# Gated heads' values of all tokens: from eight jobs inside the halves to seven half-size products in a first stage

## The chip, the cores and the metric

The kernel runs on one core of a Trainium2 chip. The metric is the time of one execution on the device in microseconds, the median of several runs. Beside the runs there is one profiled execution, from which the page and all rows below come. TensorE multiplies, ScalarE and VectorE move, split and scale data, GpSimd adds operands that lie in SBUF, and the queue of SyncE (SP) issues nearly all DMA transfers.

## The reference, cut to what matters

A decoder layer on x of 1024 tokens by 2048 (float32). One input projection feeds two head groups; their gated outputs go through one output projection, a residual and a layer norm:

```python
h = jnp.einsum('bsd,de->bse', x, w_in[l])
q_a, k_a, v_a, z_a, q_g, k_g, v_g, z_g, gk_lr = jnp.split(h, pts, axis=-1)
y_a = _swa_sink_attention(qa, ka, va, attn_sinks[l]) * jax.nn.silu(z_a)   # 16 heads of 64, window 128
gk = log_sigmoid(gk_lr @ w_gk_up[l] + b_gk[l]) / 16
o_g = _gla_chunked(q_g, k_g, v_g, gk)                    # 4 gated heads, keys of 128, values of 256
y_g = rms_norm(o_g) * gla_norm_w[l] * jax.nn.silu(z_g)
x = _layer_norm(DN_ALPHA * x + concat([y_a, y_g]) @ w_out[l], ln_g[l], ln_b[l])
```

The change touches `v_g`: columns 3328 to 4352 of the projection, 1024 tokens x 2048 inputs x 1024 outputs.

## The kernel before, in words

**Precision.** Every large product is made of three matmuls: each operand is split into a high part (`A.copy` to float32r, L112) and a low remainder (`V.tensor_tensor` subtract, L113), and high x high, high x low and low x high are summed in PSUM. A split covers 128x512 and costs one ScalarE and one VectorE instruction. Loads land in tiles `raw` (4 buffers of 512 KB); split weights live in `w_p` (8 high, 8 low), split x in `x_p` (16 high, 16 low).

**Stages.** Two halves of 512 tokens, one after the other (`half_jobs`, L491), then an output stage. In a half, x is loaded and split once and stays; `begin` (L588) does that, with the first pair of jobs and the low-rank products of the decay (`low_rank`, L307). Then 38 jobs follow in the order of `ORDER` (L42). A job of kind f (`main_f`, L165) computes one block of 128 output columns for the half's 512 tokens: 16 k steps x 3 matmuls with weights held and x moving, 128x512 each. A job of kind v (`main_v`, L177) computes the 256 value columns of one gated head: 16 k steps x 4 token blocks x 3 matmuls with x held and weights moving, 128x256 each. There are 34 jobs of kind f and 4 of kind v in a half.

**What runs beside the jobs.** A job has an evacuation and a list `later`, whose entry n is run n jobs on (`run_later`, L648). For a gated head: after its key job (`k_job`, L511) come the decays and the operands of four near levels, a chain over ScalarE, VectorE and GpSimd; after its v job the values are split out of PSUM (L523, L524) and `near`, the products of these levels (`level_products`, L346), is due at once, then `far` one job on and two `pair` steps after that. For an attention job a (`qa`): the rotary step and the scores one job on. All of it is side work in the gaps of other engines; the scheduler puts its matmuls between those of the jobs. Every second job four loads, four GpSimd operations and a store prepare sums of output weights (`weight_sums`, L627).

**The output stage** (L818 on) is itself seven half-size products over 8 k steps, with y held and 512 weight columns moving, two column halves each. Sums of y are made by GpSimd from blocks loaded again (`y_part`, L708), one product ahead.

**Order.** A scheduler orders each engine's instructions by priority (program order, moved ahead inside `high_priority`) and by its own timing model; each engine and each queue then works strictly in that order. Before, the first loads of half 0 are pinned (`load_first`, L581), use a pool of their own (`x0`), and the low-rank products of half 0 come after the first pair.

Of the kernel before, what the change touches and what calls it, by code (L numbers as in the profile page):

```python
# [41 lines left out]
ORDER = [  # L42
    "K V q0 k0 v0 a0 z0 a1 z1 g0 h0 a2 z2 q1 k1 v1 a3 z3 g1 h1 a4 z4 q2 k2 v2 a5 z5 g2 h2 a6 z6 q3 k3 v3 a7 z7 g3 h3",
    "K V q0 k0 v0 a0 z0 a1 z1 g0 h0 a2 z2 q1 k1 v1 a3 z3 g1 h1 a4 z4 q2 k2 v2 a5 z5 g2 h2 a6 z6 q3 k3 v3 a7 z7 g3 h3",
]
# [30 lines left out]
def build(ctx: ExitStack, tc, xT, xr, w_e, w_v, w_gk, w_up, b_gk, cos_d, sin_d, cst_d, sinks, wn_d, w_out, g_d, b_d, out):  # L76
# [11 lines left out]
    ap = side.enter_context(tc.tile_pool(name="ap", bufs=1))  # L88
    so = side.enter_context(tc.tile_pool(name="so", bufs=1, space=PSUM))
    sd = side.enter_context(tc.tile_pool(name="sd", bufs=3, space=PSUM))  # L90

    x0 = ExitStack()
    x0_p = x0.enter_context(tc.tile_pool(name="x0", bufs=8))


    def load(src, pool=None, pieces=1, ahead=2000):

        r = (pool or raw_p).tile([P, 2, 512], F32, name="raw", tag="raw")
        v = src.rearrange("p (u c) -> p u c", u=2)
        with tc.high_priority(ahead):  # L100
            for i in range(pieces):
                u = slice(2 * i // pieces, 2 * (i + 1) // pieces)
                ins = SP.dma_start(r[:, u], v[:, u])
                if ahead == 0:
                    tc.keep_in_program_order(ins)
        return [r[:, 0], r[:, 1]]
# [9 lines left out]
    def load_split(src, pool, tag, ahead=2000):  # L116
        out = []
        for i in range(src.shape[-1] // 1024):
            out += [split(u, pool, tag) for u in load(src[:, 1024 * i:1024 * i + 1024], ahead=ahead)]
        return out  # L120
# [40 lines left out]
    ys_d = dr_p.tile([P, 8 * T], F32, name="ysum")  # L161
    yd = [[dr_p.tile([P, 4 * T], F32, name=f"yd{H}_{q}") for q in range(4)] for H in range(2)]
# [13 lines left out]

    def main_v(w, xs):  # L177
        acc = [mm.tile([P, 2, 256], F32, name="accv", tag="mm") for _ in range(2)]
        for k in range(KT):
            wh, wl = w[k // 2]  # L180
            c = slice((k % 2) * 256, (k % 2) * 256 + 256)
            xh, xl = xs[k]
            for tb in range(NB):
                o = acc[tb // 2][:, tb % 2]
                t = slice(tb * P, tb * P + P)
                PE.matmul(o, xh[:, t], wh[:, c], start=(k == 0 and tb % 2 == 0), stop=False, skip_group_check=True)  # L186
                PE.matmul(o, xh[:, t], wl[:, c], start=False, stop=False, skip_group_check=True)  # L187
                PE.matmul(o, xl[:, t], wh[:, c], start=False, stop=(k == KT - 1), skip_group_check=True)  # L188
        return acc
# [301 lines left out]
    def half_jobs(H):  # L491
# [19 lines left out]
        def k_job(hd):  # L511
            def evac(acc):
                A.copy(c["kq", hd][:, 0], acc)
                c["dd", hd] = decays(hd, c["lr"])
                c["ws", hd] = {h: level_operand(c["kq", hd], c["dd", hd], h) for h in NEAR}
            e_job(H, E_KG + hd, evac)

        def v_job(hd):
            def evac(acc):
                v = c["v", hd] = [gp.tile([P, NB, 256], F32R, name=f"vg{i}", tag=f"vg{i}") for i in range(2)]  # L520
                for i in range(2):
                    o = slice(2 * i, 2 * i + 2)
                    A.copy(v[0][:, o], acc[i])  # L523
                    V.tensor_tensor(v[1][:, o], acc[i], v[0][:, o].bitcast(F32), ALU.subtract)  # L524
# [11 lines left out]
            jobs.append(Job([w_v[hd][:, :2048], w_v[hd][:, 2048:]], H, "v", evac, (near, far, pair, pair)))  # L536
# [15 lines left out]
        make = {"K": ka, "V": va, "q": q_job, "k": k_job, "v": v_job, "g": lambda hd: zg(hd, 0), "h": lambda hd: zg(hd, 1), "a": qa, "z": za}  # L552
        for j in ORDER[H].split():
# [27 lines left out]
    def load_first(srcs):  # L581
        rs = [(p or raw_p).tile([P, 2, 512], F32, name="raw", tag="raw") for p in (x0_p, None, None)]
        for u in range(2):
            for r, src in zip(rs, srcs):
                tc.keep_in_program_order(SP.dma_start(r[:, u], src[:, 512 * u:512 * u + 512]))
        return [[r[:, 0], r[:, 1]] for r in rs]

    def begin(H, i):  # L588
# [5 lines left out]
        if H:  # L594
            with tc.high_priority(2000):
                c["wgk"] = cp.tile([P, KT * 32], F32, name="wgk", tag="lr")
                SP.dma_start(c["wgk"], w_gk)
        for q in range(4):
            for j in range(2):
                src = xT[H, q][:, 1024 * j:1024 * j + 1024]  # L600
                if H:
                    xr += load(src)
                elif q or j:
                    xr += load(src, x0_p, 1, 0)
                if j == 0 and q % 2 == 0:
                    ws = [jobs[i + n].src[0][:, 512 * q:512 * q + 1024] for n in range(2)]
                    if H or q:
# [304 lines left out]
```

## Time and profile before

| | |
|---|---|
| median of 3 runs | 1436.53 us (1434.97 to 1437.89) |
| profiled execution, its own time | 1435.88 us |
| its span | 1433.7 us |
| TensorE busy | 1414.9 us, 99% |
| VectorE / ScalarE / GpSimd busy | 856.7 / 600.3 / 290.3 us |
| bytes moved | 222.36 MB, 155 GB/s over the span |

A row of a timeline or of the chain begins with start and length in us. A matmul's length contains its way through the array, so consecutive matmuls overlap; the distance between starts is what one costs.

### The profile page before, as it was taken

Reading aid. Unit: us, or ns where it says so; the run is one execution under the profiler, and the core shown is the slowest. Engines: PE = TensorE matmul, PEld = TensorE weight load, DVE = VectorE, ACT = ScalarE, POOL = GpSimd, SP = SyncE. Lnnn points to the kernel's source line nnn. Section 1 sums busy time; section 2 is a strip of 40 time slices with the busy share of each in tenths; the row PEclk is TensorE's granted clock in tenths of the full one; section 3 lists DMA queues with packets and bytes.
Section 4 is the critical chain, followed back from the end, with each engine's and each line's share of the span. In section 5 each row is a group of like instructions: output and inputs, shape, how many; then the busy total and the mean of one; then the engine's idle time right before and its main releaser. Section 6 shows DMA issues by size and latency. Waiting matters only on the chain.

```text
span 1433.7 us, 23435 instructions
## 1 busy us (share of the span) xinstructions
PE 1414.9 (99%) x8992; PEld 1181.0 (82%) x8992; DVE 856.7 (60%) x1481; ACT 600.3 (42%) x1279; POOL 290.3 (20%) x325
## 2 busy tenths in 40 slices
PE   8999999999999999999999999999999999999996
PEld 5888889888888976898888888988898888888885
DVE  5565556555655566565655555564566645466798
ACT  5544435435443445344435443443545324433320
POOL 0032212221311122213212221131101412122000
PEclk9999999999999999999999999999999999999998
DMA  8243344443434435543443334433325797665552
GB/s 318 86 148 128 111 147 131 135 133 107 144 131 134 133 127 175 168 157 113 159 133 123 115 131 136 138 112 118 104 95 163 239 362 230 216 218 189 172 208 117
DMA packets 99231, 222.36 MB, mean 155 GB/s; under 512 B 10800, under 2 KB 43568, under 8 KB 97968
## 3 DMA queue, kind: packets, MB, share of 16 engines
q1 hardware_dynamic: 97968, 218.78, 46.1%
q10 hardware_dynamic: 1152, 2.10, 0.4%
q8 instruction: 70, 1.15, 0.3%
q14 instruction: 41, 0.34, 0.1%
HBM read 180.47 MB, written 35.65 MB: 151 GB/s over the span
## 4 chain that ended last, share of the span: by engine, by line
PE 98%; DVE 1%; DMA 1%; ACT 0%; POOL 0%; SPq 0%; issue 0%; DVEq 0%; POOLq 0%
PE acc L172 18%; PE acc L174 18%; PE acc L173 17%; PE acco L742 7%; PE acco L743 7%; PE acco L744 7%; PE accv L186 4%; PE accv L188 4%; PE accv L187 4%; PE po L291 2%; PE pa L360 1%; PE ps L259 1%; PE ps L260 1%; PE pt L281 1%; PE lracc L310 1%; PE pg L405 1%
## 5 line engine op out<-in xcount | busy, mean ns | idle before, releaser
L113 DVE TENSOR_TENSOR wl<-raw,wh 128x512 fp32r<-128x512 f32 x440 | 331.6, 759 | 280.7 <-ACT wh L112 258.1
L112 ACT CAST wh<-raw 128x512 fp32r<-128x512 f32 x440 | 269.8, 620 | 416.9 <-PE acc L173 283.5
L172 PE MATMUL acc<-xh,wh 128*128 128x512 f32 x1088 | 429.4, 396 | 6.5 <-ACT wh L112 6.5
L174 PE MATMUL acc<-xh,wl 128*128 128x512 f32 x1088 | 427.1, 393 | 0.0
L173 PE MATMUL acc<-xl,wh 128*128 128x512 f32 x1088 | 426.9, 393 | 0.0
L172 PEld LDWEIGHTS acc<-xh,wh 128*128 128x128 f32 x1088 | 205.0, 188 | 53.8 <-ACT wh L112 8.4
L174 PEld LDWEIGHTS acc<-xh,wl 128*128 128x128 f32 x1088 | 204.8, 188 | 44.8 <-issue 1.4
L173 PEld LDWEIGHTS acc<-xl,wh 128*128 128x128 f32 x1088 | 205.0, 188 | 42.6 <-issue 2.2
L743 PE MATMUL acco<-wl,xh 128*128 128x512 f32 x416 | 161.9, 389 | 0.0
L742 PE MATMUL acco<-wh,xh 128*128 128x512 f32 x416 | 160.7, 390 | 0.2
L744 PE MATMUL acco<-wh,xl 128*128 128x512 f32 x416 | 160.8, 389 | 0.0
L186 PE MATMUL accv<-wh,xh 128*128 128x256 f32 x512 | 145.3, 284 | 0.0
L188 PE MATMUL accv<-wh,xl 128*128 128x256 f32 x512 | 145.0, 283 | 0.0
L187 PE MATMUL accv<-wl,xh 128*128 128x256 f32 x512 | 144.8, 283 | 0.0
L186 PEld LDWEIGHTS accv<-wh,xh 128*128 128x128 f32 x512 | 98.1, 192 | 1.2 <-issue 0.7
L188 PEld LDWEIGHTS accv<-wh,xl 128*128 128x128 f32 x512 | 98.1, 192 | 0.6 <-issue 0.3
L187 PEld LDWEIGHTS accv<-wl,xh 128*128 128x128 f32 x512 | 98.2, 192 | 0.5
L742 PEld LDWEIGHTS acco<-wh,xh 128*128 128x128 f32 x416 | 78.1, 188 | 17.3 <-ACT xh L112 1.3
L744 PEld LDWEIGHTS acco<-wh,xl 128*128 128x128 f32 x416 | 78.1, 188 | 16.7 <-DVE xl L113 0.4
L743 PEld LDWEIGHTS acco<-wl,xh 128*128 128x128 f32 x416 | 78.1, 188 | 15.8
L113 DVE TENSOR_TENSOR xl<-yr,xh 128x512 fp32r<-128x512 f32 x56 | 38.5, 687 | 77.4 <-ACT xh L112 76.9
L112 ACT CAST xh<-yr 128x512 fp32r<-128x512 f32 x56 | 34.6, 620 | 118.4 <-POOL yr L721 66.9
(169 smaller groups left out, 1686.7 us busy)
## 6 DMA issues: line engine op xcount, KB each, us to landing
raw<-in_w_e_dram SPq DMA_DIRECT2D x134, 512.0 KB, 3.9
yr<-yd SPq DMA_DIRECT2D x88, 256.0 KB, 4.8
raw<-in_w_v_dram SPq DMA_DIRECT2D x32, 512.0 KB, 4.2
raw<-in_w_out_dram SPq DMA_DIRECT2D x128, 128.0 KB, 2.7
td<-raw SPq DMA_DIRECT2D x32, 512.0 KB, 3.5
raw<-td SPq DMA_DIRECT2D x32, 512.0 KB, 4.6
raw<-in_w_out_dram SPq DMA_DIRECT2D x24, 512.0 KB, 4.0
raw<-in_xT_dram SPq DMA_DIRECT2D x15, 512.0 KB, 4.7
```

Of the source, the lines that this page charges most:

```text
L112: A.copy(hi, src)
L113: V.tensor_tensor(lo, src, hi.bitcast(F32), ALU.subtract)
L172: PE.matmul(acc, wh[:, c], xh, start=(k == 0), stop=False)
L173: PE.matmul(acc, wh[:, c], xl, start=False, stop=False)
L174: PE.matmul(acc, wl[:, c], xh, start=False, stop=(k == KT - 1))
L186: PE.matmul(o, xh[:, t], wh[:, c], start=(k == 0 and tb % 2 == 0), stop=False, skip_group_check=True)
L187: PE.matmul(o, xh[:, t], wl[:, c], start=False, stop=False, skip_group_check=True)
L188: PE.matmul(o, xl[:, t], wh[:, c], start=False, stop=(k == KT - 1), skip_group_check=True)
L291: x = PE.matmul(po[64 * u:64 * u + 64, a:b], vt[:, j + 1, 64 * g:64 * g + 64], pms[u][:, a2:b2], start=(len(heads) < 2), stop=(j == NB - 1 ...
L742: PE.matmul(acc, yh[:, c], wh, start=(first and k == 0), stop=False, skip_group_check=True)
L743: PE.matmul(acc, yh[:, c], wl, start=False, stop=False, skip_group_check=True)
L744: PE.matmul(acc, yl[:, c], wh, start=False, stop=(last and k == 7), skip_group_check=True)
```

## The change

The values of all four gated heads and all 1024 tokens become one matrix product ahead of the halves. It is cut in two along tokens (T0, T1), inputs (K0, K1) and columns (F0, F1), and the four blocks of the result are made from seven products of half size instead of eight, with sums of blocks as operands (Winograd's form of Strassen's scheme). In the order in which they run:

| product | x operand | weight operand | goes to |
|---|---|---|---|
| 1 | T0K0 | K0F0 | kept in u1, and stays in the banks |
| 2 | T0K1 | K1F0 | added to 1 in the same banks: values of T0, F0 |
| 7 | T0K0 - T1K0 | K0F1 + K1F1 | u7 |
| 5 | T1K0 - T1K1, kept in `xsum` | K0F0 + K0F1, kept in `wsum` | u5 |
| 6 | `xsum` - T0K0 | `wsum` + K1F1 | u1, u7, u5, and values of T1, F1 |
| 4 | T1K1 | `wsum` + K1F0 | values of T1, F0 |
| 3 | `xsum` + T0K1 | K1F1 | values of T0, F1 |

The table gives the operations of the code below. Each product is 8 k steps x 4 token blocks x 3 matmuls of 128x512. Sums are made by GpSimd, x sums one product ahead; results go to DRAM (`vd`) and come back per head and half in the key job's evacuation, where they are split from SBUF instead of PSUM. `near` moves from the v job to one job after the key job. Half 0 now begins like half 1.

```diff
-ORDER = [
-    "K V q0 k0 v0 a0 z0 a1 z1 g0 h0 a2 z2 q1 k1 v1 a3 z3 g1 h1 a4 z4 q2 k2 v2 a5 z5 g2 h2 a6 z6 q3 k3 v3 a7 z7 g3 h3",
...
+ORDER = "K V q0 k0 a0 z0 a1 z1 g0 h0 a2 z2 q1 k1 a3 z3 g1 h1 a4 z4 q2 k2 a5 z5 g2 h2 a6 z6 q3 k3 a7 z7 g3 h3"
+    vd = [[dr_p.tile([P, NB, 512], F32, name=f"vd{H}_{F}") for F in range(2)] for H in range(2)]
...
-    def main_v(w, xs):
...
@@ k_job, evac
-            e_job(H, E_KG + hd, evac)
-
-        def v_job(hd):
-            def evac(acc):
+                r = raw_p.tile([P, NB, 256], F32, name="raw", tag="raw")
+                SP.dma_start(r, vd[H][hd // 2][:, :, hd % 2 * 256:hd % 2 * 256 + 256])
                 v = c["v", hd] = [gp.tile([P, NB, 256], F32R, name=f"vg{i}", tag=f"vg{i}") for i in range(2)]
-                for i in range(2):
-                    o = slice(2 * i, 2 * i + 2)
-                    A.copy(v[0][:, o], acc[i])
-                    V.tensor_tensor(v[1][:, o], acc[i], v[0][:, o].bitcast(F32), ALU.subtract)
+                A.copy(v[0], r)
+                V.tensor_tensor(v[1], r, v[0].bitcast(F32), ALU.subtract)
...
-            jobs.append(Job([w_v[hd][:, :2048], w_v[hd][:, 2048:]], H, "v", evac, (near, far, pair, pair)))
+            e_job(H, E_KG + hd, evac, (None, near, far, pair, pair))
...
@@ begin: load_first, the pool x0 and the late low-rank products of half 0 go; both halves do
+                with tc.high_priority():
+                    low_rank(c["lracc"], c["wgk"], k, xr[k])
...
+    vo = v_st.enter_context(tc.tile_pool(name="vo", bufs=5, space=PSUM))
...
+    xsum = [vp.tile([P, T], F32, name=f"xsum{k}") for k in range(8)]
+    wsum = [vp.tile([P, 2, 512], F32, name=f"wsum{k}") for k in range(4)]
+    us = {(i, t): vp.tile([P, 512], F32, name=f"u{i}{t}") for i in (1, 5, 7) for t in range(NB)}
...
+    def v_x(i, k):
...
+        if i in (1, 2, 4):
+            a = raw(*{1: (0, 0), 2: (0, 1), 4: (1, 1)}[i], "xh")
+        elif i == 7:
+            a = raw(0, 0, "xh")
+            G.tensor_tensor(a, a, raw(1, 0, "xl"), ALU.subtract)
+        else:
+            a = xsum[k]
+            if i == 5:
+                fetch(a, block(1, 0))
+            b = raw(*{5: (1, 1), 6: (0, 0), 3: (0, 1)}[i], "xl")
+            G.tensor_tensor(a, a, b, ALU.add if i == 3 else ALU.subtract)
+        return split(a, x_p, "x")
...
+    def v_w(i, kp):
...
+        if i in (1, 2, 3):
+            r = raw(*{1: (0, 0), 2: (1, 0), 3: (1, 1)}[i])
+        elif i == 7:
+            r = raw(0, 1)
+            G.tensor_tensor(r, r, raw(1, 1), ALU.add)
+        else:
+            r = wsum[kp]
+            if i == 5:
+                fetch(r, block(0, 0).rearrange("p (u c) -> p u c", u=2))
+            G.tensor_tensor(r, r, raw(*{5: (0, 1), 6: (1, 1), 4: (1, 0)}[i]), ALU.add)
+        return [split(r[:, u], w_p, "w") for u in range(2)]
...
+    def v_collect(i, t, acc):
+        u1, u5, u7 = (us[j, t] for j in (1, 5, 7))
+        if i == 1:
+            A.copy(u1, acc)
...
+        elif i == 6:
+            V.tensor_tensor(u1, u1, acc, ALU.add)
+            V.tensor_tensor(u7, u7, u1, ALU.add)
+            o = raw_p.tile([P, 512], F32, name="raw", tag="raw")
+            V.tensor_tensor(o, u5, u7, ALU.subtract)
+            SP.dma_start(vd[1][1][:, t], o)
+            V.tensor_tensor(u5, u5, u1, ALU.subtract)
+        else:
+            o = u7 if i == 4 else u5
+            V.tensor_tensor(o, o, acc, ALU.add)
+            SP.dma_start(vd[1 if i == 4 else 0][0 if i == 4 else 1][:, t], o)
+
+    v_seq = (1, 2, 7, 5, 6, 4, 3)
...
+        for k in range(8):
+            if (i, k) not in v_xs:
+                v_xs[i, k] = v_x(i, k)
+            if k % 2 == 0:
+                wv = v_w(i, k // 2)
+            if vn + 1 < len(v_seq):
+                v_xs[v_seq[vn + 1], k] = v_x(v_seq[vn + 1], k)
+            (xh, xl), (wh, wl) = v_xs[i, k], wv[k % 2]
+            for t in range(NB):
+                c = slice(t * P, t * P + P)
+                PE.matmul(v_acc[t], xh[:, c], wh, start=(k == 0 and i != 2), stop=False, skip_group_check=True)
+                PE.matmul(v_acc[t], xh[:, c], wl, start=False, stop=False, skip_group_check=True)
+                PE.matmul(v_acc[t], xl[:, c], wh, start=False, stop=(k == 7 and i != 1), skip_group_check=True)
+        for t in range(NB):
+            v_collect(i, t, v_acc[t])
...
-        if i > 5 and i % 2 == 0 and i // 2 - 3 < 32:
-            weight_sums(i // 2 - 3)
+        if i > 3 and i % 2 == 0 and i // 2 - 2 < 32:
+            weight_sums(i // 2 - 2)
```

The pools of the side work (`ap`, `gp`, and `so`, `sd` in PSUM) open only after the first stage has closed its own, on the same memory.

## Rows read from the trace of the kernel before

**Rows 1.** busy time per engine, from the page: us (share of the span) xinstructions
```profile
PE 1414.9 (99%) x8992; PEld 1181.0 (82%) x8992; DVE 856.7 (60%) x1481; ACT 600.3 (42%) x1279; POOL 290.3 (20%) x325
```

**Rows 2.** the chain that ended last, from the page, by engine
```profile
PE 98%; DVE 1%; DMA 1%; ACT 0%; POOL 0%; SPq 0%; issue 0%; DVEq 0%; POOLq 0%
```

**Rows 3.** windows of all engines: busy us and instructions, clock, DMA share, GB/s
```profile
core 0: us, PE busy (x) PEld busy (x) DVE busy (x) ACT busy (x) POOL busy (x), PEclk, DMA share, GB/s
0.00:20.00 20.00, 13.51 (x49) 9.54 (x50) 11.93 (x19) 12.84 (x22) 1.72 (x10) 1.00 0.89 328
1140.00:1160.00 20.00, 20.00 (x90) 16.57 (x89) 10.41 (x18) 5.36 (x9) 3.11 (x2) 1.00 1.04 396
1160.00:1180.00 20.00, 20.00 (x90) 16.58 (x89) 6.35 (x10) 4.82 (x9) 4.70 (x4) 1.00 1.02 347
...
243.00:256.00 13.00, 13.00 (x146) 10.36 (x137) 9.52 (x18) 6.30 (x11) 1.48 (x2) 1.00 0.47 163
...
60.00:530.00 470.00, 470.00 (x3416) 400.22 (x3415) 277.42 (x500) 208.48 (x458) 107.56 (x131) 1.00 0.40 130
```

**Rows 4.** TensorE by line, v jobs: xcount | busy us, mean ns | idle
```profile
L186 PE MATMUL accv<-wh,xh 128*128 128x256 f32 x512 | 145.3, 284 | 0.0
```

**Rows 5.** timeline of the first v job on TensorE: start us, us
```profile
63.87 0.28 PE L186 MATMUL accv<-wh,xh 128*128 128x256 f32 x1
...
71.43 0.28 PE L186 MATMUL accv<-wh,xh 128*128 128x256 f32 x1
```

**Rows 6.** timeline of the output stage on TensorE
```profile
1140.18 0.39 PE L742 MATMUL acco<-wh,xh 128*128 128x512 f32 x1
...
1172.82 0.39 PE L742 MATMUL acco<-wh,xh 128*128 128x512 f32 x1
```

**Rows 7.** windows of the low-rank products alone: TensorE busy us (x), clock, DMA
```profile
0.00:45.00 45.00, 6.13 (x32) 1.00 0.75 271
530.00:575.00 45.00, 8.42 (x32) 1.00 0.50 166
```

**Rows 8.** timeline of the start: the first matmul
```profile
6.49 0.80 PE L172 MATMUL acc<-xh,wh 128*128 128x512 f32 x1 [6.49 <-ACT wh L112]
```

**Rows 9.** by line and shape, splits and GpSimd: busy us, mean ns | idle
```profile
L112 ACT CAST wh<-raw 128x512 fp32r<-128x512 f32 x440 | 269.8, 620 | 416.9 <-PE acc L173 283.5 <-PE accv L188 55.6 <-issue 25.1
...
L113 DVE TENSOR_TENSOR xl<-raw,xh 128x512 fp32r<-128x512 f32 x40 | 26.5, 690 | 14.1 <-ACT xh L112 14.0
...
L208 POOL TENSOR_TENSOR rs<-rs,sin 128x512 f32<-128x512 f32 x18 | 31.8, 1769 | 97.3 <-DMA rs<-rq 97.2
...
L635 POOL TENSOR_TENSOR raw<-raw 128x256 f32<-128x256 f32 x32 | 24.5, 765 | 241.6 <-DMA raw<-in_w_out_dram 227.9 <-DVE wl L113 4.6 <-DVE sza L303 4.6
...
L334 POOL TENSOR_TENSOR dd<-dd,ge 128x512 f32<-128x512 f32 x8 | 10.2, 1277 | 67.0 <-ACT ge L332 67.0
```

**Rows 10.** timeline of GpSimd and VectorE where their operations meet
```profile
796.74 0.73 POOL L637 TENSOR_TENSOR raw<-raw 128x256 f32<-128x256 f32 x1
797.55 1.07 POOL L638 TENSOR_TENSOR raw<-raw 128x256 f32<-128x256 f32 x1
...
796.04 0.69 DVE L524 TENSOR_TENSOR vg<-accv,vg 128x512 fp32r<-128x512 f32 x1 [1.43 <-ACT vg L523]
...
796.84 1.18 DVE L113 TENSOR_TENSOR wl<-raw,wh 128x512 fp32r<-128x512 f32 x1
```

**Rows 11.** timeline of a gated head: decay chain, then near products among matmuls
```profile
770.50 0.58 ACT L513 COPY kq<-acc 128x512 f32<-128x512 f32 x1
...
786.17 0.69 DVE L342 TENSOR_TENSOR w<-kq,w 128x512 f32<-128x512 f32 x1 [0.16 <-ACT w L341]
...
799.13 0.40 PE L173 MATMUL acc<-xl,wh 128*128 128x512 f32 x1
799.46 0.46 PE L360 MATMUL pa<-w 128*32 128x32 f32 x32
799.84 0.50 PE L174 MATMUL acc<-xh,wl 128*128 128x512 f32 x1
```

More of the change, by code (lines that the diff above doesn't have):

```diff
@@ L87, in build, with load @@
     cp = side.enter_context(tc.tile_pool(name="cp", bufs=1))
[L88 to L105, printed above, removed]
+    def load(src):
+        r = raw_p.tile([P, 2, 512], F32, name="raw", tag="raw")
+        with tc.high_priority(2000):
+            SP.dma_start(r, src.rearrange("p (u c) -> p u c", u=2))
         return [r[:, 0], r[:, 1]]
@@ L114, in split, with load_split @@
         return hi, lo
-    def load_split(src, pool, tag, ahead=2000):
+    def load_split(src, pool, tag):
         out = []
         for i in range(src.shape[-1] // 1024):
-            out += [split(u, pool, tag) for u in load(src[:, 1024 * i:1024 * i + 1024], ahead=ahead)]
+            out += [split(u, pool, tag) for u in load(src[:, 1024 * i:1024 * i + 1024])]
         return out
@@ L175, in main_f @@
         return accs
-    def main_v(w, xs):
[L178 to L189, printed above, removed]
     def silu2(acc, pool, tag, bufs):
@@ L579, in build @@
     parts = {}
[L581 to L586, printed above, removed]
     def begin(H, i):
@@ L593, in begin @@
         xr = []
[L594 to L597, printed above, removed]
+        with tc.high_priority(2000):
+            c["wgk"] = cp.tile([P, KT * 32], F32, name="wgk", tag="lr")
+            SP.dma_start(c["wgk"], w_gk)
         for q in range(4):
             for j in range(2):
[L600 to L604, printed above, removed]
-                if j == 0 and q % 2 == 0:
-                    ws = [jobs[i + n].src[0][:, 512 * q:512 * q + 1024] for n in range(2)]
-                    if H or q:
-                        wr = [load(w, ahead=2000 * H) for w in ws]
-                    else:
-                        xr, *wr = load_first([src] + ws)
+                xr += load(xT[H, q][:, 1024 * j:1024 * j + 1024])
+                if j == 0 and q % 2 == 0:
+                    wr = [load(jobs[i + n].src[0][:, 512 * q:512 * q + 1024]) for n in range(2)]
             for n in range(2):
@@ L646, in build @@
+    v_st.close()
+    ap = side.enter_context(tc.tile_pool(name="ap", bufs=1, reuse_waits="tile"))
+    gp = side.enter_context(tc.tile_pool(name="gp", bufs=1, reuse_waits="tile"))
+    so = side.enter_context(tc.tile_pool(name="so", bufs=1, space=PSUM, reuse_waits="tile"))
+    sd = side.enter_context(tc.tile_pool(name="sd", bufs=3, space=PSUM, reuse_waits="tile"))
     pending = []
@@ L657, in build @@
         if i in (0, n0):
-            xr0 = begin(H, i)
+            begin(H, i)
         group = [i, i + 1] if i in paired else [i]
         ws = [get(j) for j in group]
-        if jobs[i].kind == "v":
-            accs = [main_v(ws[0], ctxs[H]["x"])]
-        else:
-            accs = main_f(ws, ctxs[H]["x"])
-        if i == 0:
-            for k in range(KT):
-                low_rank(ctxs[0]["lracc"], ctxs[0]["wgk"], k, xr0[k])
+        accs = main_f(ws, ctxs[H]["x"])
         if i in (0, n0):
             evac_lr(H)
-        if i == 0:
-            x0.close()
-            gp = side.enter_context(tc.tile_pool(name="gp", bufs=1, reuse_waits="tile"))
         run_later()
```

59 lines of the change are left out of this document (42 added, 17 removed).

## The prediction

> **What bounds the kernel now.** Read the busy table first: TensorE is busy for 1414.9 of 1433.7 us, and the next engine, VectorE, for 60% [rows 1]. A modelled matmul end can hide small waits, so the chain of waits comes second: 98% of the chain that ended last is TensorE itself [rows 2]. Third, the windows: from 60 to 530 us TensorE is busy without a break, with VectorE at 277 of 470 us, ScalarE at 208 and GpSimd at 108 [rows 3]. So the time is TensorE's time, and an edit is worth what it takes from TensorE's queue, unless it makes TensorE wait. The profiled execution took 1435.88 us, 2.2 us more than its span; the median of the runs is 1436.53, 0.65 us higher. I sum against the first and add 0.65 at the end.
>
> **What goes.** Eight jobs of kind v (four heads in two halves), 16 k x 4 token blocks x 3 = 192 matmuls each, 1536 in all, of 128x256; a third of them is one row of the table by lines [rows 4]. The listed 284 ns is no price, since matmuls overlap: the price is the distance between starts. From 63.87 to 71.43 us lie 63 starts of the v job, 7.56 / 63 = 0.1200 us each [rows 5]. So 1536 x 0.1200 = 184.3 us leave TensorE.
>
> **What comes.** Seven products x 8 k x 4 token blocks x 3 = 672 matmuls with x as the held operand and 512 weight columns moving. The output stage has this very form. From 1140.18 to 1172.82 us lie 144 of its starts, 32.64 / 144 = 0.2267 us each [rows 6]. So 672 x 0.2267 = 152.3 us are added, 21.76 us a product. The net is **-32.0 us**: an eighth of the multiplications goes (23 us), and the wider operand is cheaper per column (9 us).
>
> The Trainium skill speaks against part of this: its page "TensorE: Matmul & The Clock Gate", section "Back-to-back issue gap", gives a gap of N / 2.4 + 2.5 ns for N columns, an estimate of 109.2 ns at 256 and 215.8 ns at 512; by it 167.7 us would go and 145.0 come, a net of -22.7 us. The rows of both widths lie higher, the narrow one by more, and the measurement decides.
>
> **The low-rank products of half 0.** Before, they run after the first pair in long runs; now they come between the k steps, as in half 1. The 32 of half 0 keep TensorE for 6.13 us, those of half 1 for 8.42 [rows 7]. The first half will cost what the second does: **+2.3 us** (0 to +2.3).
>
> **The start.** Before, the first matmul starts at 6.49 us, after 256 KB of x, 256 KB of weights and their split [rows 8]. The new first product needs the same amounts, so 0 us. After that one k step (2.72 us of matmuls) takes 256 KB of x, 256 KB of weights and 256 KB of x for the next product, 0.79 MB; at the 328 GB/s of the first 20 us [rows 3] that is 2.4 us. ScalarE's three splits of 0.62 us and VectorE's three of 0.69 [rows 9] fit as well. I take 0 (-1 to +2). What began at 6.49 us, half 0, now begins behind the last product; its loads then hide behind matmuls, as those of half 1 do now.
>
> **Feeding the stage: the term with the wide bounds.** A product of 21.76 us needs 16 splits on each of ScalarE (16 x 0.62 = 9.9 us) and VectorE (16 x 0.69 = 11.0), and sums or differences on GpSimd. There a 128x512 operation costs 1.277 us and a 128x256 one 0.765 [rows 9], so 0.51 per further 256 columns and 2.30 for a 128x1024 weight sum. Nothing in the trace keeps VectorE and GpSimd busy at once for long, but it shows what a meeting costs: the product with the sine table, which always meets VectorE, takes 1.769 us against 1.277 [rows 9], and a split that ran beside two GpSimd sums took 1.18 us instead of 0.69 while the next sum took 1.07 instead of 0.73; the split just before it, which reads PSUM, kept its 0.69 [rows 10]. So a meeting of two operations that read SBUF costs 0.49 us on one of them. Per product, with every split charged to GpSimd's queue (the product's own weight sums and the x sums of the next one):
> product 2: 8 x 1.277 + 16 x 0.49 = 18.1 us (3.7 to spare);
> product 7: 4 x 2.30 + 8 x 1.277 + 7.8 = 27.3 (5.5 over), product 5 the same;
> product 6: 9.2 + 7.8 = 17.0 (4.8 to spare);
> product 4: 27.3 and the 12 sums of product 6's collect that read SBUF alone, 5.9, = 33.1 (11.4 over).
> With nothing carried over, 22.4 us are late. With all of it carried over, 22.4 - 8.5 to spare - 5.9, because those 12 sums may end during product 3, leaves 8.0; and GpSimd can begin product 7's work while product 1 still runs, since it has none there. Below, a stall of 0 is possible: half the meetings may not happen. I take **+6 us**, nearer to the carried sum, because x and the split weights have room for one product ahead; 0 and 22 stay for the range.
>
> DMA is the same place seen from another side. During products 7 and 5 the loads are w7 4, x5 4, w5 4, x6 2 MiB, with 1 MiB of results stored and 0.6 of constants: 16.4 MB in 43.5 us, 376 GB/s. The output stage moved 396 and then 347 GB/s in two neighbouring windows of 20 us with TensorE busy throughout [rows 3]. At 347 these two products would be 3.7 us late; this shares its lead with GpSimd's lateness and is not added.
>
> Between products 1 and 2 the sums stay in their banks, and ScalarE copies them out in between. A bank's copy (0.62 us by the nearest row, a ScalarE pass over 128x512 [rows 9]) has the nine matmuls of the three other banks, 2.04 us, as cover, with room for two splits queued ahead of it. 0 us, at most 1. If the cover goes, the wait stands in front of all later products in TensorE's queue.
>
> **The halves without v jobs.** Removed there: 64 weight splits and 16 evacuations on both engines; added: 8 loads of 512 KB, and 8 passes of 128x1024 on each. From 60 to 530 us lie four v jobs, 92 us; without them and their 32 splits VectorE has 277 - 22 = 255 of 378 us [rows 3]: two thirds busy, no bound. Each load joins SP's queue behind the weight loads, and behind it wait the stores and the swaps of the rotary step; its values are wanted only two jobs later. The weight sums move a job earlier, and the last ones into the last pair; their first reader is the second output product, over 40 us on. The near products now follow the key job after one attention job instead of a v job. I take **+1 us** in all (0 to +27, below).
>
> **Sum.** 1435.9 - 32.0 + 2.3 + 0 + 6 + 1 = 1413.2, and 0.65 more against the median: **1414 us**.
>
> **Rivals.**
> *The stage is fed without a stall.* For it: in the output stage, of the same form, TensorE stays busy at 396 GB/s [rows 3]. Against it: a product there has twice as many matmuls per x block, so x work comes half as densely, and GpSimd is used for 3 of 20 us. Time: 1436.5 - 32.0 + 2.3 = 1407.
> *VectorE and GpSimd take whole turns.* Then a meeting costs a full split, 0.69: products 7 and 5 take 19.4 + 11.0 = 30.4 us (8.7 over each), product 4 19.4 + 11.0 + 8.3 = 38.7 (16.9 over), products 2 and 6 21.2 and 20.2 (2.0 to spare together); less the 8.3 that may end later, 24.0 us late. Time: 1407 + 24 = 1431. For it: the 1.18 us row. Against it: the price there is 0.49 and not 0.69.
> The Trainium skill, page "SBUF — State Buffer", section "Who interferes with whom", has this rule: a VectorE instruction with two SBUF inputs and a GpSimd instruction that reads SBUF exclude each other, and the later one blocks fully. The rows agree on which instructions meet, and not that the whole instruction is lost.
> *The halves lose their cover: slower.* The decay chain of a head, from the copy of the keys at 770.50 to the end of the last near operand at 786.17 + 0.69, takes 16.4 us on ScalarE, VectorE and GpSimd [rows 11]. Today a v job of 23 us covers it; then only an attention job with its side work does, 13.0 us [rows 3]. If TensorE's order puts the near products right behind that job, it waits 3.4 us a head, 8 x 3.4 = 27 us: 1414 + 27 = 1441, slower than now. It decides from 2.8 us a head ((1436.5 - 1414) / 8) on. Against it: the order is finer than jobs. Today a run of 32 near products stands between two matmuls of the next job [rows 11], so products that are late are placed later.
>
> **Chances.** Forecast (1408 to 1421) 0.58; fed without a stall (1405 to 1408) 0.20; whole turns (1421 to 1436) 0.15; halves uncovered (1430 to 1441) 0.07. The range 1404 to 1430 holds the first two and over half of the third. A measurement of this kernel tells 0.2%, 2.9 us, from no change. Faster takes the first two, 0.12 of the third and 0.01 of the last, 0.91; same 0.02 of the third and 0.02 of the last, 0.04; slower 0.01 and 0.04, 0.05.
>
> **What will show it.** No matmul of 128x256 into accv, and 672 of 128x512 at 0.227 us between starts; a first stage of some 155 to 165 us. If the supply term is right, TensorE's waits lie in products 7, 5 and 4 and end on a split of a weight or x tile whose releaser is GpSimd; GpSimd is over 80% busy there and VectorE's splits average 0.9 us or more. If they end on a DMA, the bandwidth was the bound. In the halves TensorE has no wait ahead of the products into pa; waits of 3 us there mean the third rival. A stage under 150 us, or waits between products 1 and 2 of more than 1 us, would prove steps of mine wrong.

## The result, and the profile after

The changed kernel takes 1524.23 us (median of 3 runs, 1522.11 to 1527.0) against 1436.53: a ratio of 1.0611, 95% interval 1.0596 to 1.0625. It is 87.7 us **slower**; 1414 was forecast. The profiled execution took 1524.23 us, its span 1522.3.

The busy row, the granted clock in 40 slices and the chain of waits, from the page of the changed kernel [rows 1, 2]:

```profile
PE 1416.3 (93%) x8128; PEld 1133.0 (74%) x8128; DVE 941.6 (62%) x1545; ACT 624.6 (41%) x1335; POOL 384.3 (25%) x373
...
PE   3877679999999999999999999999999799999996
...
PEclk7899979999999999999999999999999899999998
...
PE 77%; DVE 6%; DMA 3%; ACT 2%; issue 2%; POOL 1%; SPq 0%; DVEq 0%; ACTq 0%; POOLq 0%
```

TensorE is no longer the whole chain: 77% instead of 98%. Its row shows where: in the first six slices (38 us each), and once more in slice 32. The busy sum is no guide, since a matmul at the lower clock counts for longer.

The first stage in windows [rows 3] (columns as there):

```profile
0.00:20.00 20.00, 8.92 (x20) 6.56 (x21) 7.25 (x11) 7.69 (x12) 1.72 (x10) 0.88 0.90 316
20.00:40.00 20.00, 6.14 (x17) 4.33 (x17) 5.69 (x10) 4.84 (x8) 0.00 (x0) 0.61 0.90 319
...
100.00:120.00 20.00, 11.37 (x40) 8.29 (x39) 8.53 (x10) 4.11 (x7) 14.49 (x8) 0.83 0.80 267
120.00:140.00 20.00, 14.94 (x52) 9.76 (x50) 11.38 (x8) 6.61 (x13) 16.84 (x11) 0.91 0.36 121
140.00:160.00 20.00, 12.58 (x49) 8.82 (x50) 7.45 (x10) 7.87 (x15) 7.92 (x6) 1.00 0.11 36
...
180.00:200.00 20.00, 1.94 (x10) 1.29 (x8) 13.44 (x23) 1.37 (x3) 3.12 (x2) 0.64 0.48 160
```

At first the DMA engines are full (0.90) and everything else is busy for less than half of the time. From 140 to 160 us no engine is full and the loads run at 36 GB/s, yet TensorE still waits for ScalarE, which is itself busy for 7.9 of 20 us. That reads as queues waiting for each other, not as a resource that is used up. What TensorE waits for, up to 254 us (us in total, times, longest):

```profile
PE accv L696 <- ACT xh L98: 46.2, 15, 13.9
PE accv L696 <- ACT wh L98: 24.1, 2, 18.1
```

The first matmul is on time [rows 8], and the half 0 jobs begin at 253.51 (TensorE's timeline):

```profile
6.01 2.07 PE L696 MATMUL accv<-wh,xh 128*128 128x512 f32 x4 [6.01 <-ACT wh L98]
...
253.51 0.40 PE L159 MATMUL acc<-xh,wh 128*128 128x512 f32 x1
```

So the stage takes 247.5 us. Against the v jobs that went, 247.5 - 184.3 = 63.2 us of the loss lie in the stage; 24.5 are left for the halves and the output. One shift between the two has to be known: 20 of the 32 low-rank matmuls of half 0 run inside product 3, four at a time, 1.07 us for each four. They make up 5.4 of the 5.8 us by which product 3 exceeds 21.8; it has no wait.

```profile
228.94 1.05 PE L283 MATMUL lracc<-raw,wgk 128*32 128x512 f32 x4
```

The length of each product, in the order of the stage, from the start of its first matmul to that of the next product's (the last: to its own last matmul), for every kernel with a stage. The starts are read to 0.1 us, so a length is good to 0.1; 21.8 is TensorE's own time, to which low-rank matmuls come in p3 (none in e5 and e7, 8 in e10, 16 to 24 in the others):

```
run                     p1    p2    p7    p5    p6    p4    p3   sum   time
changed kernel         57.7  21.8  37.9  36.4  40.1  25.8  27.6  247  1524.2
e1 kept tiles late     48.3  21.8  32.9  37.2  36.3  24.4  28.8  230  1507.9
e2 own block           59.4  21.9  39.9  39.5  34.7  21.8  30.1  247  1528.7
e3 GpSimd in order     56.2  36.5  47.1  36.8  41.5  35.5  27.5  281  1561.5
e5 by hand             24.3  21.7  21.8  28.5  31.7  26.7  21.5  176  1468.4
e6 keys earlier        58.4  21.8  38.0  36.5  39.4  25.7  28.3  248  1506.9
e7 e5 and e6           24.1  21.8  21.8  28.0  31.8  26.7  21.5  176  1443.9
e8 + keys, GpSimd      23.2  21.8  21.8  26.0  31.8  25.6  28.7  179  1440.3
e9 weights on VectorE  23.6  21.8  22.7  28.6  23.5  21.7  27.6  169  1426.2
e10 all on VectorE     24.7  21.7  23.1  25.4  21.8  21.8  23.9  162  1423.4
e11 loads held         24.0  21.8  21.8  21.7  30.7  27.5  36.1  184  1445.6
e12 arithmetic held    31.1  24.2  21.8  31.9  27.5  23.3  35.1  195  1454.4
```

**Product 1.** SP's queue in the changed kernel (start us, us, line, operation):

```profile
2.59 0.43 SPq L604 DMA_DIRECT2D yr<-in_xT_dram  x1
...
4.04 4.52 SPq L604 DMA_DIRECT2D xsum<-in_xT_dram  x5
...
10.35 2.28 SPq L604 DMA_DIRECT2D xsum<-in_xT_dram  x3
13.00 2.35 SPq L604 DMA_DIRECT2D wsum<-in_w_v_dram  x4
...
29.25 3.83 SPq L604 DMA_DIRECT2D yr<-in_xT_dram  x7
```

The tiles that are kept for product 5 (xsum, wsum: 4 MiB) were issued before most x blocks of product 1 (yr). The rate is near the 328 GB/s of the forecast, 319; it went to what nobody wanted yet.

**Products 7 and 5.** GpSimd, then ScalarE (brackets: idle before, and what ended it):

```profile
94.61 1.29 POOL L619 TENSOR_TENSOR yr<-yr 128x512 f32<-128x512 f32 x1
95.86 5.17 POOL L650 TENSOR_TENSOR wsum<-wsum,raw 128x1024 f32<-128x1024 f32 x2
102.32 2.67 POOL L650 TENSOR_TENSOR wsum<-wsum,raw 128x1024 f32<-128x1024 f32 x1 [1.28 <-DVE wl L99]
104.95 1.26 POOL L619 TENSOR_TENSOR yr<-yr 128x512 f32<-128x512 f32 x1
```

```profile
130.98 0.62 ACT L98 CAST wh<-wsum 128x512 fp32r<-128x512 f32 x1 [2.27 <-PE accv L698]
131.50 0.61 ACT L98 CAST xh<-xsum 128x512 fp32r<-128x512 f32 x1
135.37 0.62 ACT L98 CAST wh<-wsum 128x512 fp32r<-128x512 f32 x1 [3.26 <-PE accv L698]
135.89 0.61 ACT L98 CAST xh<-xsum 128x512 fp32r<-128x512 f32 x1
```

The differences of x that product 7 wants next (L619) stand behind weight sums of products 5 and 6 (L650), which wait for a split. In product 5 ScalarE's next instruction is a weight split for product 6, which waits until TensorE gives its buffer back; the x split for the coming k step stands behind it. So a k step runs through a ring: TensorE, weight split, x split, VectorE, TensorE, in 4.4 us (from 131.50 to 135.89) instead of 2.7.

**Between products 6 and 4** TensorE waits 18.06 us. SP's row in the table of waits, and GpSimd's:

```profile
SPq L670 <- DVE raw L669: 20.6, 3, 20.1
```

```profile
196.88 4.66 POOL L650 TENSOR_TENSOR wsum<-wsum,raw 128x1024 f32<-128x1024 f32 x2 [40.46 <-DMA raw<-in_w_v_dram]
```

SP holds a store of product 6's block, which VectorE makes once product 6 has ended; product 4's weights stand behind it. This wait is the last part of p6 in the table: product 6 itself runs without a stall.

**The halves.** TensorE's waits behind the stage, of the changed kernel; the kernel before has no wait there:

```profile
PE pa L333 <- DVE w L315: 8.9, 6, 2.7
PE po L444 <- DVE on L413: 6.3, 2, 3.3
PE po L264 <- DVE pm L256: 2.9, 1, 2.9
```

The last two rows lie at the end of the second half, where the wait costs twice: from 1202 to 1225 us the granted clock is 0.63 on average, and from 1219.9 to 1223.3 us the output stage's matmuls start 0.43 us apart, at the lower of the two levels (1.2 GHz).

```profile
1202.00:1225.00 23.00, 16.09 (x62) 11.97 (x63) 11.22 (x31) 5.56 (x16) 6.85 (x8) 0.63 0.43 135
```

### The profile page after: what moved, and what is told of

It reads as the page before. It is cut to its first block, busy times and chain, and to the rows that moved or that the text cites. A ratio compares the mean times of both kernels' runs of the same rounds, so it can differ in the third digit from the quotient of the medians.

```text
span 1522.3 us, 22157 instructions
## 1 busy us (share of the span) xinstructions
PE 1416.3 (93%) x8128; PEld 1133.0 (74%) x8128; DVE 941.6 (62%) x1545; ACT 624.6 (41%) x1335; POOL 384.3 (25%) x373
## 4 chain that ended last, share of the span: by engine, by line
PE 77%; DVE 6%; DMA 3%; ACT 2%; issue 2%; POOL 1%; SPq 0%; DVEq 0%; ACTq 0%; POOLq 0%
PE acc L159 15%; PE acc L161 14%; PE acc L160 14%; PE acco L798 6%; PE acco L796 6%; PE acco L797 6%; PE po L264 2%; PE accv L696 2%; PE accv L698 2%; PE accv L697 2%; DVE wl L99 1%; PE ps L232 1%; PE ps L233 1%; DMA yr<-yd 1%; DVE dd L316 1%
## 5 line engine op out<-in xcount | busy, mean ns | idle before, releaser
L99 DVE TENSOR_TENSOR wl<-raw,wh 128x512 fp32r<-128x512 f32 x408 | 317.8, 788 | 180.1 <-ACT wh L98 174.1
L98 ACT CAST wh<-raw 128x512 fp32r<-128x512 f32 x408 | 246.6, 618 | 270.3 <-PE acc L160 195.8
L160 PEld LDWEIGHTS acc<-xl,wh 128*128 128x128 f32 x1088 | 204.6, 188 | 41.9 <-issue 1.8
L696 PE MATMUL accv<-wh,xh 128*128 128x512 f32 x224 | 94.6, 430 | 70.3 <-ACT xh L98 46.2
L99 DVE TENSOR_TENSOR xl<-yr,xh 128x512 fp32r<-128x512 f32 x88 | 68.4, 781 | 132.9 <-ACT xh L98 131.9
L98 ACT CAST xh<-yr 128x512 fp32r<-128x512 f32 x88 | 54.0, 620 | 212.5 <-POOL yr L775 71.5
L696 PEld LDWEIGHTS accv<-wh,xh 128*128 128x128 f32 x224 | 45.3, 203 | 89.0 <-ACT xh L98 54.3
L697 PE MATMUL accv<-wl,xh 128*128 128x512 f32 x224 | 94.2, 421 | 0.5 <-DVE wl L99 0.4
L796 PEld LDWEIGHTS acco<-wh,xh 128*128 128x128 f32 x416 | 78.7, 189 | 16.3
L580 POOL TENSOR_TENSOR raw<-raw 128x256 f32<-128x256 f32 x32 | 26.1, 814 | 224.5 <-DMA raw<-in_w_out_dram 163.5
L698 PE MATMUL accv<-wh,xl 128*128 128x512 f32 x224 | 80.2, 416 | 1.6 <-DVE xl L99 1.5
L775 POOL TENSOR_TENSOR yr<-yr 128x512 f32<-128x512 f32 x32 | 44.2, 1383 | 145.7 <-DMA yr<-yd 107.7
```

Source lines behind the costliest of these rows:

```text
L98: A.copy(hi, src)
L99: V.tensor_tensor(lo, src, hi.bitcast(F32), ALU.subtract)
L160: PE.matmul(acc, wh[:, c], xl, start=False, stop=False)
L696: PE.matmul(v_acc[t], xh[:, c], wh, start=(k == 0 and i != 2), stop=False, skip_group_check=True)
L697: PE.matmul(v_acc[t], xh[:, c], wl, start=False, stop=False, skip_group_check=True)
L698: PE.matmul(v_acc[t], xl[:, c], wh, start=False, stop=(k == 7 and i != 1), skip_group_check=True)
```

## The experiments

Two theories: **order** (each engine works its queue off in order, and what is not wanted yet stands ahead of what is), and **supply** (DMA, VectorE and GpSimd can't do the work of a product in 21.8 us whatever the order). Each kernel below was run once, e10 five times, beside runs of the kernel before (1434.98 to 1438.22 us). The repeats of one kernel here lie within 5 us of each other, so smaller differences between single runs say nothing. The code is shortened.

**e1: the kept tiles later**

```diff
-        with tc.high_priority(2000):
-            SP.dma_start(t, src)          # xsum, wsum
+        tc.keep_in_program_order(SP.dma_start(t, src))
```

> Edit: the twelve tiles that are first wanted in product 5 (8 of x, 4 of weights, 4 MiB) are loaded in program order, beside product 7, and no more at the head of SP's queue. Theory 'order of the queues' (what is not wanted yet stands ahead of what is): product 1 loses about 20 of its 36 us of waiting, the run takes about 1500 to 1508 us. Rival 'supply' (DMA, VectorE and GpSimd cannot bring a product of operands in 21.8 us, whatever the order): the waits only move to products 2 and 7, where the same 4 MiB now load, and the time stays at 1520 to 1528.

1507.88 us, 16.3 less. Product 1 lost 9 us and product 7 5: not the 20, but the sign and the time of the order theory. Of the eight kept x tiles two still load during product 1 (at 33.6 and 41.9 us), and in SP's queue the constants and the weights of the next products still stand ahead of x.

**e2: product 6's block in tiles of its own**

```diff
-            o = raw_p.tile([P, 512], F32, name="raw", tag="raw")
+            o = vp.tile([P, 512], F32, name="o6", tag="o6", bufs=4)
```

> Edit: the block that product 6 sends to DRAM is built in four tiles of its own and no more in a buffer of the raw weights. Theory 'order of the queues': the 18 us wait between products 6 and 4 comes from product 4's raw weights, which wait for these buffers, so behind a store that waits for VectorE's collecting; it goes, 1505 to 1509 us. Rival 'supply': GpSimd's sums and VectorE's splits for product 4 are late by themselves (the forecast's 5 to 11 us), then at most a third of it goes, 1517 to 1521.

1528.72 us: a miss for both. The wait of 18 us is gone (product 4 starts 0.2 us after product 6's last matmul), and the stage is as long as it was: product 6 takes 34.7 us, 13 of them lost inside it, and products 1, 7, 5 and 3 are each 1.7 to 3.1 us longer. ScalarE in product 6:

```profile
171.23 0.62 ACT L98 CAST wh<-wsum 128x512 fp32r<-128x512 f32 x1 [4.70 <-PE accv L698]
171.75 0.61 ACT L98 CAST xh<-xsum 128x512 fp32r<-128x512 f32 x1
175.48 0.62 ACT L98 CAST wh<-wsum 128x512 fp32r<-128x512 f32 x1 [3.11 <-PE accv L698]
```

Product 4's weights now arrive early, so their splits stand ahead of product 6's x splits, and the ring of product 5 has come to product 6. By these rows the store that held SP up had kept that ring away; no run shows this apart.

**e3: GpSimd alone in the order of the program**

```diff
-            G.tensor_tensor(a, a, b, ALU.add if i == 3 else ALU.subtract)
+            tc.keep_in_program_order(G.tensor_tensor(a, a, b, ALU.add if i == 3 else ALU.subtract))
```

(and so for the three other lines with sums and differences.)

> Edit: GpSimd's differences and sums of x stand in its queue in the order of the program, so that the weight sums of products 5 and 6 do not overtake those of x that TensorE wants first. Theory 'order of the queues': products 7 and 5 lose most of their 31 us of waiting, 1496 to 1504 us. Rival 'whole turns of VectorE and GpSimd': the number of meetings is the same in any order, 15 to 17 us of waiting stay in products 7 and 5, 1508 to 1516. Rival 'slots': the order was not what made them late, 1520 to 1528.

1561.52 us, 37 slower: no theory had that. GpSimd's waits from 80 to 270 us:

```profile
POOL xsum L626 <- DMA yr<-in_xT_dram: 63.9, 12, 10.4
POOL wsum L650 <- DMA raw<-in_w_v_dram: 31.0, 1, 31.0
POOL yr L619 <- DMA yr<-in_xT_dram: 13.8, 3, 9.6
```

In a fixed order it waits for x loads that SP has put behind others. Here an order on one queue that the other queues don't share was worse than none.

**e4: the halves and the output alone**

```diff
-    v_seq = (1, 2, 7, 5, 6, 4, 3)      # and the loop over it
-    SP.dma_start(r, vd[H][hd // 2][:, :, hd % 2 * 256:hd % 2 * 256 + 256])
+    SP.dma_start(r, w_out[2 * H + hd // 2, 0].rearrange(...)[:, :, hd % 2 * 256:hd % 2 * 256 + 256])
```

> Edit: the first stage of seven products is left out (the values are loaded from other data, the output is not the reference's), so the halves and the output stage run alone. If the stage has the whole loss, the halves cost what they did before, 1436.5 - 184.3 + 2.3 = 1254.5 us, with a start of up to 8 us more since the first loads have no cover: 1253 to 1263. If the halves lose as well, as the gaps between the starts of their matmuls say (+27): 1280 to 1290.

1290.31 us, 0.3 above the second case. Of the 35.8 over 1254.5, the start has 4.6: the first half job stands at 11.1 us instead of 6.5, behind a wait of 9.1 for the x of the low-rank products; those of half 1 wait 1.4 more. TensorE's waits `pa`, `po` and `po` of the three rows above are 10.5 + 7.9 + 2.7 = 21.1 us here. The other 8.7 have no single row: shorter waits are 1.8 of them, and from 978 to 994 us, behind the waits at the end, the granted clock is 0.65. So the halves lose by themselves.

**e5: the whole stage ordered by hand.** The same work, in a loop over the 56 k steps; each load, sum, split, copy and store of it is held to the written order on its queue (`pin`). In outline:

```diff
+    for s in range(-8, 62):
+        x_add(s + 6), w_add(s + 6)               # GpSimd
+        sx[s + 4] = pin_split(x), sw[s + 4] = pin_split(w)
+        x_load(s + 8), w_load(s + 8)             # SP
+        ...                                      # TensorE: step s
+        # a product's collect: one block a step, its store two steps later
```

> Edit: the first stage's work is the same in number and size, but its order on every queue is written out: at each k step of TensorE the loads stand 8 steps ahead, GpSimd's sums 6, the splits of x and of the weights 4; the kept tiles load beside product 7, the block of product 6 that goes to DRAM has tiles of its own, and the constants load in product 2. Theory 'order of the queues': the waits come from instructions that stand ahead of what TensorE wants first, on SP, GpSimd and ScalarE at once, so mending one of them (the two runs before) only moves the wait. The stage takes 155 to 175 us instead of 247, the run 1430 to 1452. Rival 'supply' (GpSimd and VectorE shut each other out): products 7, 5 and 4 keep 8, 8 and 15 us of waiting at least, the stage takes over 185 us, the run 1462 or more.

1468.40 us, 55.8 less, and the stage takes 176 us instead of 247 (some 5 of the difference because no low-rank matmul is left in it). The stage lies 1 us above the range of the order theory, far from that of its rival; the time lies in the rival's. Products 5, 6 and 4 keep 6.7 + 9.9 + 4.9 = 21.5 us, and this kernel added a wait of 6.0 itself, since the low-rank weights now load last and the low-rank products come behind the stage. So both have a part: 55.8 + 6.0 = 62 us went with the order, and 21.5 stay in the order by hand. What these are, e8 to e10 ask.

**e6: query and key jobs two jobs earlier**

```diff
-"K V q0 k0 a0 z0 a1 z1 g0 h0 a2 z2 q1 k1 a3 z3 g1 h1 a4 z4 q2 k2 a5 z5 g2 h2 a6 z6 q3 k3 a7 z7 g3 h3"
+"K V q0 k0 a0 z0 a1 z1 g0 h0 q1 k1 a2 z2 a3 z3 g1 h1 q2 k2 a4 z4 a5 z5 g2 h2 q3 k3 a6 z6 a7 z7 g3 h3"
```

> Edit: in TensorE's list of jobs the query and key jobs of heads 1, 2 and 3 stand two jobs earlier, so that a head's near products and pairs have two jobs more before its gate jobs. The stage is as in the changed kernel. Theory 'the last head's pairs come too late' (near one job later than before, and the last two jobs are one group): the 16 us at the end of the second half and half of the 8 us in front of the near products go, 1500 to 1510 us. Rival 'the decay chain is too long for one attention job': the wait follows the key job wherever it stands, 1518 to 1528.

1506.89 us, 17.3 less. All waits in front of `pa` are gone, and those at the end of the second half are 0.5 and 0.2 us. There, too, one attention job stands between a key job and its near products, so the decay chain is not too long for one: what follows the key job had too few jobs until the gate jobs.

**e7: both**

> Edit: the stage's order by hand and the earlier key jobs together. If the two causes are apart, the gains add: by the order theory 1408 to 1432 us, less than before or near it; by the supply rival 1440 or more.

1443.91 us: 80.3 less, where the two apart gave 55.8 + 17.3 = 73.1. The two causes are apart, but the time is not in the order theory's range: it stays above the kernel before, where the supply rival had it.

**e8, e9, e10: who adds.** All three have e7's order, with the low-rank weights loaded with the constants. e8 adds on GpSimd; then

```diff
-            G.tensor_tensor(a, a, b, ALU.add)      # weights: e9, e10
+            V.tensor_tensor(a, a, b, ALU.add)
-            G.tensor_tensor(a, a, b, ...)          # x: e10
+            V.tensor_tensor(a, a, b, ...)
```

> Edit: the kernel of the last run (order by hand, key jobs earlier) with the 256 KB of low-rank weights loaded with the constants and no more behind the stage's last load. TensorE waited 6.5 us for them: 1436 to 1439 us. All sums on GpSimd: products 5, 6 and 4 keep the 21.5 us of waiting above 21.76 us each.

> Edit: as the run beside it, with the weight sums on VectorE and the sums of x still on GpSimd. Theory 'VectorE and GpSimd take whole turns': a product with both sums takes 11.0 + 5.3 us on VectorE and 10.3 on GpSimd, 26.6 together, so products 5 and 6 keep some 8 to 12 us of waiting: 1424 to 1430 us. Rival 'a meeting costs 0.49 us, and GpSimd's queue alone was too long': GpSimd then has 10.3 + 3.9 us a product, so no waiting: 1415 to 1420.

> Edit: as the runs beside it, with all sums on VectorE, none on GpSimd. Theory 'whole turns': nothing shuts VectorE out any more; it has 16 splits of 0.69 us, 8 sums of x of 0.69 and 4 of weights of 1.33, 21.9 us a product against TensorE's 21.8, so the stage keeps 0 to 6 us of waiting and takes 156 to 163 us: 1415 to 1422 us, faster than the kernel before by 1.0 to 1.5%. Rival 'the loads bound products 7 and 5' (16.4 MB in 43.5 us): the waits stay whatever engine adds, 1430 to 1437.

e8: 1440.31, 1.3 above its range; products 5, 6 and 4 keep 18.1 us. e9: 1426.22, in the range of the whole turns; these three keep 8.5. e10, five runs: **1423.41 us** (1422.05 to 1426.22) against 1436.59, a ratio of 0.9911, 95% interval 0.9894 to 0.9927. That is 1.4 above its range and 0.9% under the kernel before; the stage takes the 162 us that were expected. The same sums, VectorE by line and shape from 72 to 130 us, first e8, then e10 (busy us, mean ns | idle), with GpSimd's of e8 between:

```profile
L617 DVE TENSOR_TENSOR wl<-wsum,wh 128x512 fp32r<-128x512 f32 x16 | 29.8, 1898 | 0.1
L617 DVE TENSOR_TENSOR xl<-xsum,xh 128x512 fp32r<-128x512 f32 x15 | 28.3, 1921 | 0.0
...
L667 POOL TENSOR_TENSOR wsum<-wsum,raw 128x1024 f32<-128x1024 f32 x11 | 30.4, 2769 | 3.6 <-issue 1.9 <-DMA raw<-in_w_v_dram 1.0 <-DVE wl L617 0.7
L662 POOL TENSOR_TENSOR xsum<-xsum,yr 128x512 f32<-128x512 f32 x15 | 25.3, 1706 | 1.0 <-DMA yr<-in_xT_dram 1.0
```

```profile
L617 DVE TENSOR_TENSOR wl<-wsum,wh 128x512 fp32r<-128x512 f32 x22 | 14.2, 689 | 0.0
L667 DVE TENSOR_TENSOR wsum<-wsum,raw 128x1024 f32<-128x1024 f32 x11 | 13.5, 1224 | 3.4 <-DMA raw<-in_w_v_dram 3.4
```

Beside a full GpSimd queue a split takes 1.9 us instead of 0.69, 32 of them in 58 us, and GpSimd does 26 operations in the same time: they take turns. One turn of e8:

```profile
110.78 2.81 POOL L667 TENSOR_TENSOR wsum<-wsum,raw 128x1024 f32<-128x1024 f32 x1
111.29 2.85 DVE L617 TENSOR_TENSOR xl<-xsum,xh 128x512 fp32r<-128x512 f32 x1
```

The sum ends at 113.59 us, the split at 114.14, 0.55 us later. So it is with 25 of the 31 splits that begin in this stretch: each begins while a GpSimd operation runs and ends 0.55 us behind that operation's end, whatever its length. The other six meet no running one and take 0.68. The windows of product 6 in e8 and in e10:

```profile
98.40:130.00 31.60, 24.00 (x97) 17.33 (x96) 31.60 (x18) 15.63 (x28) 29.02 (x14) 1.00 0.50 170
```

```profile
100.70:122.30 21.60, 21.60 (x97) 17.86 (x96) 21.57 (x33) 14.41 (x26) 0.00 (x0) 1.00 0.69 227
```

VectorE is full in both, with 18 instructions in 31.6 us and with 33 in 21.6. A reader who sees only e8's busy share would say that VectorE has too much to do; giving it more made the product faster. TensorE's longest waits in e10, without those in front of the first matmul (5.8) and in product 7 (0.9):

```profile
PE accv L723 <- DVE wl L617: 3.3, 1, 3.3
PE pt L254 <- POOL s L251: 2.7, 1, 2.7
PE ps L232 <- DVE al L342: 2.0, 4, 0.6
```

The first, in product 5, goes back to a load: VectorE's sum there waited 2.87 us for the weights, with the DMA engines at 378 GB/s over the product. So the turns are shown by products 6 and 4, which lose 10.0 and 3.8 us in e8 and nothing in e10. Product 5 loses 4.3 in e8 and still 3.7 in e10, then to the loads.

**e11, e12: which queue's order.** e8 with only the loads and stores held to the written order, and with only the arithmetic held (there the stores stay held as well, and the loads are told to go early).

> Edit: as run e8 (order by hand, sums on GpSimd), but only the loads and stores are held to the written order; the splits, sums and copies are written in that order and may be moved. Theory 'SP's order decides': the arithmetic engines follow the loads, so the time stays within 8 us of e8's 1440: 1434 to 1448 us. Rival 'ScalarE's and GpSimd's orders decide' (weight splits of the next product ahead of the x splits of this one): the k steps of 4.4 us come back in products 5 and 6, 1455 to 1475.

> Edit: as run e8, but only the splits, sums and copies are held to the written order; the loads go as early as their buffers allow, as in the changed kernel. Theory 'SP's order decides': the kept tiles load in product 1 again, whose waiting of 20 us comes back, and x loads come late for GpSimd's fixed order as in the run with GpSimd's order alone: 1465 to 1490 us. Rival: the loads follow their buffers anyway, 1440 to 1450.

1445.60 us, inside the range of SP's theory; and 1454.41, between its two cases. Each half held to the order loses little (5.3 us, near what two single runs can differ by, and 14.1) when the program itself is written in it: it seems that the scheduler follows the program unless a load is told to go early. Held arithmetic with free loads is the dearer one: the kept tiles load in product 1 again, from 7.6 us on (product 1: 31.1 us). With e3 it suggests that arithmetic in a fixed order is only as good as the loads' order.

## Why the prediction was wrong

The forecast missed by 110 us, and the rows above divide this among three of its terms: some 36 at the start, 47 in feeding the stage (53 instead of 6), 27 in the halves (28 instead of 1; by subtraction).

**The bound, what goes and what comes: right.** Product 2 of the changed kernel, which nothing disturbs, takes 21.8 us. Two of its matmuls in TensorE's timeline, 96 starts apart, give 21.89 / 96 = 0.228 us, one row's price being 0.2267 [rows 6]:

```profile
63.66 0.50 PE L696 MATMUL accv<-wh,xh 128*128 128x512 f32 x1
...
85.55 0.39 PE L696 MATMUL accv<-wh,xh 128*128 128x512 f32 x1
```

The low-rank products of half 0 keep TensorE for 8.42 us, as forecast [rows 7]; between products 1 and 2 TensorE loses nothing, as forecast.

**"The start: 0 us": failed, +36.** Product 1 takes 57.7 us instead of 21.8. The step priced what one k step needs at the rate of the DMA engines. It didn't count what stands ahead of it on SP's queue, though the diff shows it: the kept tiles' loads have the same early priority as the first x block, and no buffer that they would wait for. The forecast itself counted these 4 MiB in products 7 and 5. e1 gives 9 us back; e5, with the constants and the next weights out of the way as well, takes 24.3 us.

**"Feeding the stage: +6": the step that failed, in two ways.** It added up each engine's work per product and let unfinished work carry over, as if an idle engine took whatever could be done next. (1) The queues are in order, and their orders differ. In the changed kernel that cost 62 us in all (e5), the start included. No single change of e1 to e3 gives it back; the order written out for all queues does (e5), and with the program in that order SP's queue alone nearly does (e11). ScalarE's queue was never held alone. (2) Even in a good order the term is 18 to 21 us (e8, e5). The price of a meeting, 0.49 us from one overlap [rows 10], was that of a short GpSimd operation that met one split. Back to back it is 1.2 us on the split (1.90 - 0.69) and some 0.43 on GpSimd (1.706 against 1.277 [rows 9]).

The right price stood in the trace of the kernel before. All 40 splits there that take over 1 us begin beside a running GpSimd operation and end 0.55 us behind its end. The split of rows 10 does so too: it met an operation of 0.73 us, so there was little to wait for. Beside the longer product with the sine table a split took 1.78:

```profile
599.71 1.81 POOL L208 TENSOR_TENSOR rs<-rs,sin 128x512 f32<-128x512 f32 x1 [22.68 <-DMA rs<-rq]
...
600.29 1.78 DVE L113 TENSOR_TENSOR wl<-raw,wh 128x512 fp32r<-128x512 f32 x1
```

So the rival **"VectorE and GpSimd take whole turns"**, given 24 us and 0.15, was right on the mechanism, though it charged a split to GpSimd where the longer wait is the split's; and what the prediction said against the Trainium skill's page "SBUF — State Buffer", section "Who interferes with whom", falls. The rule there is an exclusive lock for a VectorE instruction with two SBUF inputs and a GpSimd one that reads SBUF; e8's rows agree: in the turn, a split waits until the GpSimd instruction has ended. e9 alone doesn't decide: its 8.5 us hold a wait for loads that e10 has too.

**The DMA side** ("3.7 us late at 347 GB/s"): near it in e10, where TensorE waits 0.9 us in product 7 and 3.3 in product 5. In the changed kernel it can't be seen, since 4 MiB of these loads had gone to product 1.

**"The halves: +1 us": failed.** The changed kernel loses 24.5 us outside the stage, some 28 if the low-rank matmuls in product 3 are counted back and the forecast +2.3 is taken off. The prediction saw that near products follow one attention job instead of a v job and looked for a wait of the decay chain. 8.9 us are waits in front of these products. It missed that far, pair and pair move one job as well, and that the last two jobs are one group, so that the last pair of the second half comes when no job is left to cover it. The third rival thus had the sign and, by luck, the size (27); its mechanism, a decay chain too long for one attention job, is not what the runs show (e6). e6 takes back 17.3. The other 10 or so stay open: about as much as TensorE still waits behind the stage in e6 (10.1 us, in waits of at most 2.7), the longest in the attention's products; no run took these away one by one.

**The sum of the forecast** doesn't hold for the changed kernel. e10 at 1423.4 lies inside the range of 1404 to 1430, but it is another kernel, with other queues, another order of jobs and its sums on VectorE, so it doesn't confirm the terms. The signs named to watch came out mixed: the waits did end on splits, and the splits averaged 0.9 to 1.1 us; but GpSimd was 66, 67 and 56% busy in products 7, 5 and 4, not over 80. That last sign spoke for order.

## What to carry to other kernels

A stage in which several engines are busy for most of the time has to be planned as queues: for every instruction that is told to go early, write down what stands behind it and what it waits for, on SP, ScalarE and GpSimd alike. When TensorE waits while no engine and no DMA is full, look for a ring of in-order queues; mend all of them at once, because mending one gave 16 us of 62 here (e1), moved the wait (e2) or added to it (e3). When two engines may exclude each other, price a meeting from the longest overlaps of the trace, not from one short one. When job lists lose a kind of job, recount the distance of everything that was hung on it, the end of the list first.

## What the runs showed of the hardware

- VectorE and GpSimd, both with two SBUF inputs and full queues, take turns (e8): a split that begins beside a running GpSimd sum ends 0.55 us behind the sum's end. On average a split of 0.69 us takes 1.90 and a GpSimd sum of 128x512 1.71 instead of 1.28, and moving all sums to VectorE shortened product 6 from 31.8 to 21.8 us. VectorE adds 128x1024 in 1.22 us (e10); GpSimd takes 2.77 while VectorE is full (e8).
- Waiting costs twice. In the changed kernel, from 20 to 40 us, with waits of up to 13.9 us, TensorE's granted clock was 0.61, and behind a wait of 5.5 us in product 7 its matmuls start 0.43 us apart, at the lower of its two levels (1.2 GHz), instead of 0.23:

```profile
106.91 0.80 PE L696 MATMUL accv<-wh,xh 128*128 128x512 f32 x1 [5.50 <-ACT xh L98]
107.50 0.63 PE L697 MATMUL accv<-wl,xh 128*128 128x512 f32 x1
107.93 0.63 PE L696 MATMUL accv<-wh,xh 128*128 128x512 f32 x1
```
